# A decoder block in one kernel: residual rows tied to the block sums, two operand sums split by VectorE, split left operands of two more FFN2 products, another token order in the last product

## The chip, the cores and the metric

One core of one Trainium2 chip. The metric is device time of one launch in microseconds (us); the kernel was run three times before the change. Names: TensorE (PE) multiplies, VectorE (DVE), ScalarE (ACT) and GpSimd (POOL) do elementwise work, SyncE (SP) issues nearly all DMAs. PSUM is the memory that TensorE writes its products to.

## The reference, cut to what matters

```python
x = layer_norm(ALPHA * x + gate1 * mixer(...), ln1_g, ln1_b)      # x: 1024 tokens x 1024, float32
...
h = x * (1 + scale2) + shift2                                     # 1024 x 1024
u = h @ ffn_w_up                                                  # 1024 x (2 * 2816): gate and value halves
u = causal_dwconv(u, ffn_conv) + ffn_conv_b                       # 3 taps per channel
a = silu(u[:, :2816]) * u[:, 2816:]
y = a @ ffn_w_down                                                # 1024 x 1024
out = layer_norm(ALPHA * x + gate2 * y, ln2_g, ln2_b)
```

The mixer (gated DeltaNet and GLA heads, two thirds of the program before the FFN) is not touched by the change.

## The kernel before, in words

**Arithmetic.** Each float32 matmul is made of three matmuls on parts: an operand is split into a rounded high part `hi` (a cast by ScalarE) and a low part `lo` = value − hi (a subtraction by DVE or GpSimd). `hi*lo`, `lo*hi` and `hi*hi` are summed in PSUM. Both FFN multiplications are block products of Winograd's kind: seven products with the numbers 1 to 7 take the place of eight, and operands and results are sums and differences of blocks.

**FFN1** (`w_up`). Channels come in 22 blocks `f` of 128; each block has the seven products, each 12 matmuls of 128x512. The activations' sums S1 to S4 (for products 5, 6, 7, 3) are made once and split once, into `s1h/s1l`, `s2h/s2l`, `s3h/s3l`, `s4h/s4l` (`s_rows`, `split_s`): S1 and S2 by ScalarE and DVE, S3 and S4 by ScalarE and GpSimd. The weights' sums are made and split per block by the generator `weights(f)`: tiles `vq` (value part), `wst` (gate part), split into `vh/vl` by `split_q`; product 4's weight sum `wq[f]` is a cell of `acc`, for f = 0 the tile `B22` of product 3, so that its sum comes after product 3's split. `carry(f, i)` takes what a product leaves in PSUM to the next: copies by ScalarE (`p1_`, `p4_`, `p5_`, `u2_`), sums by DVE (`add_p1` at L1456, L1477, L1479, L1481), the convolution `conv` (ScalarE L1400, two DVE instructions L1403), SiLU (L1460) and the product with the gate (L1461).

**Between the two.** After every second block the generator `sums(j)` makes the left operands of FFN2 from a pair of blocks and stores them to DRAM: products 1, 5 and 3 whole (`dS`), products 6, 7, 2 and 4 in two parts by `put_split` (`dSp`, L1410 ScalarE, L1411 DVE or GpSimd). `residual_rows(n)` scales 16 half tiles (128 tokens x 512) of the first LayerNorm's output for the last residual: load (L1447), two DVE instructions (L1449, L1450), store (L1451). Two cells of `acc` take turns.

**FFN2** (`w_down`). Products in the order 1, 5, 6, 3, 7, 2, 4; each has 11 entries (`entry`) of a left and a right operand, in a ring of eight slots of `aH/aL`, and for every entry four token tiles of three matmuls. The right operand is loaded (`R0`, `R1`, `bt`), cast by ScalarE (L1614) and split by DVE (L1615). A left operand that was stored in two parts is loaded right into its slot; one that was stored whole is loaded to `st`, cast by ScalarE (L1617) and split by GpSimd (L1618). `collect` and `done` (L1666 to L1670) take the results out of PSUM, `ln2` normalises them. In the last product, token tiles are gone through one after the other; tiles 0 and 1 lie in one PSUM tile, 2 and 3 in another, the last in two halves of 256 columns.

**What sets the order.** TensorE's order is the program's (`manual_schedule`). The order on DVE, ScalarE, GpSimd and SP is set by a scheduler that places each instruction where it expects its inputs, so code that is written late in the loop may stand early in a queue: the 16 pairs of residual instructions, written one per block from f = 4 on, all ran between 739.9 and 840.6 us. Each engine works through its queue in order.

## Time and profile before

| | |
|---|---|
| three runs | 1469.51, 1470.5, 1473.1 us; median 1470.5 |
| profiled execution | 1465.25 us, its span 1463.5 us |
| busy | PE 1333.3 us (91%), DVE 1013.6 (69%), ACT 591.9 (40%), POOL 577.1 (39%) |
| mean granted clock of TensorE | 0.949 of full |

The span is the time from the first to the last instruction of the profiled execution; FFN1 proper begins at some 740 us and FFN2 at 1210 us of it. A timeline row has start and duration in us, engine, line and operation, tiles (out<-in) and, in brackets, how long the engine had been idle and what ended that. Lines are those of the kernel before; in the change they lie 2 to 11 lines further down (L1352 becomes L1363, L1449 L1451, L1456 L1458, L1614 L1616).

### The profile page before, as it was taken

How to read it: one execution, taken by the hardware profiler on the slowest of the kernel's cores; microseconds unless marked ns; L12 is line 12 of the kernel's file. 1: busy time of each engine (PE TensorE's matmuls, PEld its weight loads, DVE VectorE, ACT ScalarE, POOL GpSimd, SP SyncE). 2: the span in 40 equal slices, each digit the busy share in tenths (PEclk: the TensorE clock that was granted, in tenths of full speed). 3: DMA queues.
4: the chain of work that ended last, by engine and by line, in shares of the span. 5: the costliest groups of instructions: out<-in, count | busy, mean ns of one | idle time of the engine just before them, and what ended most of it. 6: DMA issues, size and time to landing. Idle time of an engine off the chain costs nothing.

```text
span 1463.5 us, 19001 instructions
## 1 busy us (share of the span) xinstructions
PE 1333.3 (91%) x6662; PEld 1059.5 (72%) x6662; DVE 1013.6 (69%) x1756; ACT 591.9 (40%) x957; POOL 577.1 (39%) x383
## 2 busy tenths in 40 slices
PE   6796999999998999999957799999999997799995
PEld 4564777777787777777846587777888775688875
DVE  7885954587458334874587888878788878832777
ACT  4356222233234432532653354544445445333221
POOL 2674211121116865442352544444544435612006
PEclk9888999999999998999988999999999998899998
DMA  9546212131204554252324643334444329775773
GB/s 317 150 150 203 71 25 57 32 72 55 67 9 122 167 186 137 93 187 89 114 87 150 202 129 99 115 118 137 137 137 137 113 81 351 233 241 165 263 242 116
DMA packets 192406, 203.39 MB, mean 139 GB/s; under 512 B 29748, under 2 KB 124848, under 8 KB 192310
## 3 DMA queue, kind: packets, MB, share of 16 engines
q1 hardware_dynamic: 192021, 201.12, 43.2%
q8 instruction: 53, 0.87, 0.2%
q10 hardware_dynamic: 288, 1.05, 0.2%
q14 instruction: 44, 0.35, 0.1%
HBM read 147.04 MB, written 55.09 MB: 138 GB/s over the span
## 4 chain that ended last, share of the span: by engine, by line
PE 53%; DVE 19%; issue 9%; DMA 8%; POOL 6%; ACT 4%; SPq 0%; POOLq 0%; DVEq 0%; ACTq 0%
PE up L1281 13%; PE pp L622 6%; PE pp L623 5%; PE pp L624 5%; PE up L1633 4%; PE up L1634 4%; PE up L1632 4%; DMA vq<-in_ffn_w_up 3%; DVE ob L1403 2%; DMA K<-in_w_ada 1%; PE dn L864 1%; DVE mac L236 1%; DVE vl L1306 1%; POOL vl L1306 1%; POOL wlo L158 1%
## 5 line engine op out<-in xcount | busy, mean ns | idle before, releaser
L622 PE MATMUL pp<-aH,wlo 128*128 128x512 f32 x432 | 191.1, 442 | 8.7 <-DVE ob L651 6.9
L158 POOL TENSOR_TENSOR wlo<-wst,whi 128x1024 fp32r<-128x1024 f32 x50 | 125.5, 2510 | 153.9 <-ACT whi L157 152.5
L623 PE MATMUL pp<-aL,whi 128*128 128x512 f32 x432 | 176.5, 409 | 0.0
L624 PE MATMUL pp<-aH,whi 128*128 128x512 f32 x432 | 176.4, 408 | 0.0
L1306 POOL TENSOR_TENSOR vl<-vq,vh 128x512 fp32r<-128x512 f32 x44 | 73.3, 1666 | 175.0 <-ACT vh L1305 164.5
L1632 PE MATMUL up<-aL,aH 128*128 128x512 f32 (+1 forms) x304 | 119.5, 393 | 19.2 <-ACT aH L1617 11.4
L1633 PE MATMUL up<-aH,aL 128*128 128x512 f32 (+1 forms) x304 | 119.3, 392 | 8.5 <-POOL aL L1618 8.5
L1403 DVE SCALAR_TENSOR_TENSOR ob<-up,colC,ob 128x1023 f32<-128x1023 f32 (+1 forms) x88 | 112.2, 1276 | 20.8 <-ACT ob L1400 20.2
L1634 PE MATMUL up<-aH 128*128 128x512 f32 (+1 forms) x304 | 118.7, 391 | 0.0
L622 PEld LDWEIGHTS pp<-aH,wlo 128*128 128x128 f32 x432 | 84.9, 196 | 30.8 <-DVE ob L651 5.8
L624 PEld LDWEIGHTS pp<-aH,whi 128*128 128x128 f32 x432 | 84.7, 196 | 20.6
L623 PEld LDWEIGHTS pp<-aL,whi 128*128 128x128 f32 x432 | 85.7, 198 | 14.5 <-issue 0.5
L157 ACT CAST whi<-wst 128x1024 fp32r<-128x1024 f32 x50 | 52.3, 1047 | 83.4 <-PE pp L624 28.1
L1618 POOL TENSOR_TENSOR aL<-st,aH 128x512 fp32r<-128x512 f32 x33 | 55.5, 1698 | 76.4 <-ACT aH L1617 76.4
L1400 ACT ACTIVATE ob<-up,colC 128x1024 f32<-128x1024 f32 x44 | 53.0, 1207 | 80.6 <-DVE up L1479 47.7
L1615 DVE TENSOR_TENSOR aL<-R,aH 128x512 fp32r<-128x512 f32 x63 | 47.2, 757 | 54.5 <-ACT aH L1614 54.3
L1632 PEld LDWEIGHTS up<-aL,aH 128*128 128x128 f32 x304 | 58.9, 194 | 32.6 <-ACT aH L1617 12.3
L1281 PE MATMUL up<-aH,vl 128*128 128x512 f32 x176 | 70.9, 403 | 11.7 <-DVE vl L1306 11.0
L1614 ACT CAST aH<-R 128x512 fp32r<-128x512 f32 x63 | 39.0, 621 | 102.2 <-PE up L1634 88.4
L1633 PEld LDWEIGHTS up<-aH,aL 128*128 128x128 f32 x304 | 58.8, 194 | 20.8 <-POOL aL L1618 9.3
L1281 PE MATMUL up<-aH,wlo 128*128 128x512 f32 x176 | 70.7, 401 | 1.9 <-ACT ob L1469 1.0
L1281 PE MATMUL up<-aL,vh 128*128 128x512 f32 x176 | 70.4, 400 | 0.0
(519 smaller groups left out, 3476.4 us busy)
## 6 DMA issues: line engine op xcount, KB each, us to landing
wst<-in_w_in SPq DMA_DIRECT2D x28, 512.0 KB
K<-in_w_ada SPq DMA_DIRECT2D x48, 256.0 KB, 2.9
wst<-in_ffn_w_up SPq DMA_DIRECT2D x22, 512.0 KB, 4.4
vq<-in_ffn_w_up SPq DMA_DIRECT2D x44, 256.0 KB, 4.0
dS<-ob SPq DMA_DIRECT2D x33, 256.0 KB, 2.1
R<-in_ffn_w_down SPq DMA_DIRECT2D x33, 256.0 KB, 5.5
st<-dS SPq DMA_DIRECT2D x33, 256.0 KB, 4.7
wada<-in_w_ada SPq DMA_DIRECT2D x8, 1024.0 KB, 8.7
```

The costliest lines, as they stand in the source:

```text
L158: eng.tensor_tensor(lo, st, hi.bitcast(F32), op=ALU.subtract)
L622: PE.matmul(pp, lo[:, k, :], aH[:, k, sl], start=(k == 0), stop=False)
L623: PE.matmul(pp, hi[:, k, :], aL[:, k, sl], start=False, stop=False)
L624: PE.matmul(pp, hi[:, k, :], aH[:, k, sl], start=False, stop=(k == NK - 1))
L1281: PE.matmul(o, w[:, k, :], a, start=flags[0], stop=flags[1], skip_group_check=not first_)
L1306: eng.tensor_tensor(lo, q, hi.bitcast(F32), op=ALU.subtract)
L1400: S.activation(t, cb, AF.Identity, bias=w(3), scale=w(2))
L1403: V.scalar_tensor_tensor(t[:, sh:], cb[:, :T - sh], w(j), t[:, sh:], op0=ALU.mult, op1=ALU.add)
L1618: G.tensor_tensor(lo[:, HS[0]], s, hi[:, HS[0]].bitcast(F32), op=ALU.subtract)
L1632: PE.matmul(pb, l_hi, r_lo, start=new, stop=False, skip_group_check=i not in (1, 5, 2))
L1633: PE.matmul(pb, l_lo, r_hi, start=False, stop=False, skip_group_check=i not in (1, 5, 2))
L1634: PE.matmul(pb, l_hi, r_hi, start=False, stop=(j == NJ - 1), skip_group_check=i not in (1, 5, 2))
```

## The change

Six edits. (1) In `weights(0)` the weight sum of product 4 gets a `vq` tile of its own and is made and split ahead of product 3's split; the call of `weights(0)` is moved ahead of `h2_of(NT - 2)`. (2) S3 and S4 are split by DVE, and their casts and splits are issued after the last cast and split of S1 and S2. (3) The two residual instructions of a half tile are issued after the sum of product 3 (`anchor`) of the latest block. (4) Products 1 and 5 are stored in two parts, product 6 whole; the order in `sums` follows from that. (5) The rows of gamma and beta of the last LayerNorm are loaded in product 3's place of the loop, not ahead of FFN2. (6) The last product takes the token tiles in the order 0, 2, 1, 3.

```diff
         split_q(f, 6, B12, V)
         yield
+        wq[f] = t4_ if f else ft([P, 4, P], "vq", 3)
+        if f == 0:
+            V.tensor_tensor(wq[f], st[:, KH[1], :], B12, op=ALU.subtract)
+            split_q(f, 4, wq[f], V)
         split_q(f, 3, B22)
         yield
-        wq[f] = t4_ if f else B22
-        V.tensor_tensor(wq[f], st[:, KH[1], :], B12, op=ALU.subtract)
+        if f:
+            V.tensor_tensor(wq[f], st[:, KH[1], :], B12, op=ALU.subtract)
         V.tensor_tensor(B12, B12, st[:, KH[0], :], op=ALU.subtract)
         split_q(f, 7, B12)
...
     with tc.manual_schedule(engines={PE.engine}):
         load_w(0)
-        h2_of(NT - 2)
-        product(1, 1)
         ahead = weights(0)
         next(ahead)
         next(ahead)
+        h2_of(NT - 2)
+        product(1, 1)
         next(ahead)
-        next(ahead, None)
-        split_q(0, 4, wq[0], V)
...
         for i in (5, 6):
-            s_rows(i, 0, 2, V)
-            s_rows(i, 2, 3, V)
-            s_rows(i, 3, 4, V)
-        s_rows(3, 0, 4, G)
-        for r0, r1 in ((0, 3), (3, 4)):
-            s_rows(7, r0, r1, G)
+            for r0, r1 in ((0, 2), (2, 3), (3, 4)):
+                split_last = s_rows(i, r0, r1)
+        next(ahead, None)
+        for i, rows in ((3, ((0, 4),)), (7, ((0, 3), (3, 4)))):
+            for r0, r1 in rows:
+                with tc.issue_after(split_last[0].ins), tc.issue_after(split_last[1].ins):
+                    s_rows(i, r0, r1)
...
-    dS = {i: dram.tile([NJ, P, 512], F32, name=f"dS{i}") for i in (1, 5, 3)}
-    dSp = {i: [dram.tile([NJ, P, 512], F32, name=f"dS{i}{s}") for s in "hl"] for i in (6, 7, 2, 4)}
+    dS = {i: dram.tile([NJ, P, 512], F32, name=f"dS{i}") for i in (6, 3)}
+    dSp = {i: [dram.tile([NJ, P, 512], F32, name=f"dS{i}{s}") for s in "hl"] for i in (1, 5, 7, 2, 4)}
...
-        nc.sync.dma_start(dS[1][j], a11)
         put_split(4, j, a22, V)
         yield
-        put_split(2, j, a12, G)
+        put_split(1, j, a11, V)
         V.tensor_tensor(a22, a21, a22, op=ALU.add)
-        nc.sync.dma_start(dS[5][j], a22)
         V.tensor_tensor(a21, a11, a21, op=ALU.subtract)
         yield
+        put_split(5, j, a22, G)
         V.tensor_tensor(a11, a22, a11, op=ALU.subtract)
-        put_split(6, j, a11, G)
+        nc.sync.dma_start(dS[6][j], a11)
         yield
         put_split(7, j, a21, G)
+        yield
+        put_split(2, j, a12, G)
...
-        V.tensor_tensor(r, r, g1h[0], op=ALU.mult)
-        V.tensor_tensor(r, r, b1h[0], op=ALU.add)
+        with tc.issue_after(anchor[0].ins):
+            V.tensor_tensor(r, r, g1h[0], op=ALU.mult)
+            V.tensor_tensor(r, r, b1h[0], op=ALU.add)
...
-            V.tensor_tensor(v[:, 0, :], v[:, 0, :], u2_, op=ALU.add)
+            anchor[0] = V.tensor_tensor(v[:, 0, :], v[:, 0, :], u2_, op=ALU.add)
...
-    g2r, b2r = rows_of(2, ln2_g[0], ln2_b[0])
+    ln2_rows = []
...
+                if i == 3 and j == 0:
+                    ln2_rows.extend(rows_of(2, ln2_g[0], ln2_b[0]))
...
-        for t in range(4):
+        for t in (0, 2, 1, 3):
```

The order on the engines moves with it, at three places.

DVE at the start of FFN1, before; `vl_6338` is the low half for product 4's weights, `s1l` and `s2l` those of S1 and S2, L1449 and L1450 residual rows:

```order
L1343 TENSOR_TENSOR vq_6275<-vq_6275,wst_6230 128x512
L1352 TENSOR_TENSOR s1l_6341<-ob,aH 128x512
L1243 TENSOR_TENSOR gate<-ob,gate 128x512
L1352 TENSOR_TENSOR s1l_6341<-gate,aH 128x512
L1244 TENSOR_TENSOR ob<-ob 128x512
L1449 TENSOR_TENSOR ob<-ob,g1h_7006 128x512
L1244 TENSOR_TENSOR ob<-gate,ob 128x512
L1306 TENSOR_TENSOR vl_6338<-vq_6276,vh_6337 128x512
L1245 TENSOR_TENSOR ob<-ob 128x512
L1450 TENSOR_TENSOR ob<-ob,b1h_7009 128x512
L1352 TENSOR_TENSOR s2l_6343<-ob,s2h_6342 128x512
```

The same place in the change; `vl_6330` is now the low half for product 4, `wst_6529` the gate weights of f = 2:

```order
L1347 TENSOR_TENSOR vq_6275<-vq_6275,wst_6230 128x512
L1243 TENSOR_TENSOR ob<-ob 128x512
L1363 TENSOR_TENSOR s1l_6337<-ob,aH 128x512
L1242 TENSOR_TENSOR gate<-gate 128x512
L1458 TENSOR_TENSOR up_6314<-up_6314,ob 128x512
L1333 TENSOR_TENSOR vq_6440<-vq_6440,wst_6236 128x512
L1244 TENSOR_TENSOR ob<-ob 128x512
L1243 TENSOR_TENSOR gate<-ob,gate 128x512
L1363 TENSOR_TENSOR s1l_6337<-gate,aH 128x512
L1245 TENSOR_TENSOR ob<-ob 128x512
L1333 TENSOR_TENSOR vq_6525<-vq_6525,wst_6529 128x512
L1244 TENSOR_TENSOR ob<-gate,ob 128x512
```

The split of product 4 stands in the row ahead of these; the residual rows are gone; the weight sums L1333 of f = 1 and f = 2 have come in ahead of the S2 splits; then S3 and S4 follow on DVE:

```order
L1363 TENSOR_TENSOR s2l_6339<-ob,s2h_6338 128x512
L1336 TENSOR_TENSOR vq_6440<-vq_6441,vq_6440 128x512
L1363 TENSOR_TENSOR s3l_6342<-ob,aL 128x1536
L1363 TENSOR_TENSOR s3l_6342<-gate,aL 128x512
L1346 TENSOR_TENSOR ob<-wst_6236,vq_6440 128x512
L1363 TENSOR_TENSOR s4l_6341<-ob,s4h_6340 128x2048
L1306 TENSOR_TENSOR vl_6477<-vq_6440,vh_6476 128x512
```

They stood in GpSimd's queue before.

DVE at the end of a block in the middle of FFN1, before; L1333 is the next weights' sum, L1456 `add_p1`, whose result TensorE waits for:

```order
L1403 SCALAR_TENSOR_TENSOR ob<-up_7384,colC,ob 128x1023
L1403 SCALAR_TENSOR_TENSOR ob<-up_7384,colC,ob 128x1022
L1333 TENSOR_TENSOR vq_7697<-vq_7697,wst_7701 128x512
L1456 TENSOR_TENSOR up_7508<-up_7508,ob 128x512
L1403 SCALAR_TENSOR_TENSOR ob<-up_7368,colC,ob 128x1023
```

In the change, with the residual rows L1451 and L1452 of that block:

```order
L1458 TENSOR_TENSOR up_7677<-up_7677,ob 128x512
L1333 TENSOR_TENSOR vq_7849<-vq_7849,wst_7853 128x512
L1403 SCALAR_TENSOR_TENSOR ob<-up_7519,colC,ob 128x1023
L1306 TENSOR_TENSOR vl_7757<-vq_7711,vh_7756 128x512
L1403 SCALAR_TENSOR_TENSOR ob<-up_7519,colC,ob 128x1022
L1433 TENSOR_TENSOR ob<-ob 128x512
L1336 TENSOR_TENSOR vq_7711<-vq_7712,vq_7711 128x512
L1479 TENSOR_TENSOR up_7695<-up_7695,ob 128x512
L1451 TENSOR_TENSOR ob<-ob,g1h_7009 128x512
L1463 TENSOR_TENSOR ob<-ob 128x1024
L1346 TENSOR_TENSOR ob<-wst_7715,vq_7711 128x512
L1452 TENSOR_TENSOR ob<-ob,b1h_7012 128x512
```

The sum stands ahead of L1333 in all blocks but f = 2, 3, 4 and 21 (before, it did in about every second one), and the residual rows behind the sum of product 3.

ScalarE at the start of FFN2, before; L1400 is the convolution of the last block, L1614 the right operands' cast, L1617 the left ones':

```order
L1460 ACTIVATE ob<-ob 128x1024
L1400 ACTIVATE ob<-up_9479,colC 128x1024
L1614 CAST aH<-R_9623 128x512 x3
L1400 ACTIVATE ob<-up_9463,colC 128x1024
L1614 CAST aH<-R_9623 128x512 x3
L1460 ACTIVATE ob<-ob 128x1024
L1617 CAST aH<-st_9626 128x512
L1617 CAST aH<-st_9633 128x512
```

In the change:

```order
L1400 ACTIVATE ob<-up_9509,colC 128x1024
L1400 ACTIVATE ob<-up_9491,colC 128x1024
L1616 CAST aH<-R_9654 128x512 x6
L1462 ACTIVATE ob<-ob 128x1024
L1616 CAST aH<-R_9654 128x512 x2
```

The left operands' casts are gone from here, and both activations stand ahead of the first right operand.

## Rows read from the trace of the kernel before

**Rows 1.** Waits of TensorE, 640 to 1464 us: line, what it waited for, total, times, longest.

```profile
PE up L1281 <- DVE up L1456: 15.3, 5, 7.4
PE up L1632 <- ACT aH L1617: 11.4, 2, 10.1
PE up L1281 <- DVE vl L1306: 11.0, 1, 11.0
PE up L1633 <- POOL aL L1618: 8.5, 2, 7.9
PE up L1632 <- DVE ob L1666: 7.8, 3, 5.7
PE up L1281 <- ACT ob L1471: 6.5, 1, 6.5
PE up L1281 <- POOL s4l L1352: 3.9, 1, 3.9
```

**Rows 2.** Windows: length; busy PE, PEld, DVE, ACT, POOL; granted clock, DMA share, GB/s.

```profile
752.70:758.30 5.60, 5.49 (x12) 3.81 (x12) 3.01 (x6) 3.28 (x3) 5.60 (x1) 0.50 0.17 48
919.00:998.00 79.00, 78.28 (x337) 62.76 (x336) 63.41 (x67) 39.62 (x56) 37.78 (x23) 1.00 0.39 127
1220.00:1252.00 32.00, 30.18 (x121) 24.03 (x121) 29.61 (x30) 14.87 (x27) 20.50 (x13) 0.90 1.02 371
```

**Rows 3.** Timeline of TensorE at the start of FFN1.

```profile
752.76 0.80 PE L1281 MATMUL up<-aH,vl 128*128 128x512 f32 x1 [10.98 <-DVE vl L1306]
...
768.89 0.79 PE L1281 MATMUL up<-s4l,vh 128*128 128x512 f32 x1 [3.86 <-POOL s4l L1352]
...
773.83 0.49 PE L1281 MATMUL up<-aL,vl 128*128 128x512 f32 x1 [0.65 <-ACT ob L1473]
...
788.94 0.77 PE L1281 MATMUL up<-s4h,vl 128*128 128x512 f32 x1 [6.54 <-ACT ob L1471]
```

**Rows 4.** Timeline of DVE at the start of FFN1.

```profile
744.20 0.68 DVE L1306 TENSOR_TENSOR vl<-vq,vh 128x512 fp32r<-128x512 f32 x1
...
755.03 0.68 DVE L1352 TENSOR_TENSOR s2l<-ob,s2h 128x512 fp32r<-128x512 f32 x1
...
764.50 4.88 DVE L1450 TENSOR_TENSOR ob<-ob,b1h 128x512 f32<-128x512 f32 x1
...
782.48 0.69 DVE L1449 TENSOR_TENSOR ob<-ob,g1h 128x512 f32<-128x512 f32 x1 [2.63 <-DMA ob<-ax]
```

**Rows 5.** Timelines of GpSimd and ScalarE at the start of FFN1.

```profile
749.47 9.58 POOL L1352 TENSOR_TENSOR s3l<-ob,aL 128x1536 fp32r<-128x1536 f32 x1 [6.35 <-ACT aL L1351]
...
763.88 4.95 POOL L1352 TENSOR_TENSOR s4l<-ob,s4h 128x2048 fp32r<-128x2048 f32 x1
...
752.52 1.05 ACT L157 CAST whi<-wst 128x1024 fp32r<-128x1024 f32 x1 [0.97 <-DMA wst<-in_ffn_w_up]
```

**Rows 6.** Timeline of DVE at the end of a block.

```profile
896.45 2.20 DVE L1333 TENSOR_TENSOR vq<-vq,wst 128x512 f32<-128x512 f32 x1 [3.56 <-DMA vq<-in_ffn_w_up]
```

**Rows 7.** Groups of DVE: the two residual instructions; count, busy, mean ns, idle before.

```profile
L1450 DVE TENSOR_TENSOR ob<-ob,b1h 128x512 f32<-128x512 f32 x16 | 18.1, 1130 | 0.1
...
L1449 DVE TENSOR_TENSOR ob<-ob,g1h 128x512 f32<-128x512 f32 x16 | 14.2, 887 | 15.6 <-DMA ob<-ax 15.6
```

**Rows 8.** Timelines of ScalarE and DVE at the start of FFN2.

```profile
1209.67 0.62 ACT L1614 CAST aH<-R 128x512 fp32r<-128x512 f32 x1 [4.67 <-DMA R<-in_ffn_w_down]
...
1212.53 1.20 ACT L1400 ACTIVATE ob<-up,colC 128x1024 f32<-128x1024 f32 x1
...
1219.13 2.63 ACT L1617 CAST aH<-st 128x512 fp32r<-128x512 f32 x4 [0.55 <-DMA st<-dS]
...
1213.76 1.28 DVE L1403 SCALAR_TENSOR_TENSOR ob<-up,colC,ob 128x1023 f32<-128x1023 f32 x1 [0.41 <-ACT ob L1400]
```

**Rows 9.** Timeline of DVE at the end of the program.

```profile
1450.26 0.42 DVE L1666 TENSOR_TENSOR ob<-up,gate 128x256 f32<-128x256 f32 x1 [0.75 <-PE up L1634]
...
1454.98 0.42 DVE L1666 TENSOR_TENSOR ob<-up,gate 128x256 f32<-128x256 f32 x1 [3.19 <-PE up L1634]
```

More of the change, by code (lines that the diff above doesn't have):

```diff
@@ L1347, in build, with s_rows @@
     parts_s = {}
-    def split_s(i, src, rows, eng):
-        hi, lo = parts_s[i]
-        S.copy(hi[:, rows, :], src)
-        eng.tensor_tensor(lo[:, rows, :], src, hi[:, rows, :].bitcast(F32), op=ALU.subtract)
-    def s_rows(i, r0, r1, eng):
+    def s_rows(i, r0, r1):
         rows = slice(r0, r1)
@@ L1361, in s_rows @@
             src = acc[:, 4 + r0:4 + r1, HS[i == 5]]
-        split_s(i, src, rows, eng)
+        hi, lo = parts_s[i]
+        return (S.copy(hi[:, rows, :], src),
+                V.tensor_tensor(lo[:, rows, :], src, hi[:, rows, :].bitcast(F32), op=ALU.subtract))
     with tc.manual_schedule(engines={PE.engine}):
         load_w(0)
-        h2_of(NT - 2)
-        product(1, 1)
         ahead = weights(0)
@@ L1448, in residual_rows @@
         yield
-        V.tensor_tensor(r, r, g1h[0], op=ALU.mult)
-        V.tensor_tensor(r, r, b1h[0], op=ALU.add)
+        with tc.issue_after(anchor[0].ins):
+            V.tensor_tensor(r, r, g1h[0], op=ALU.mult)
+            V.tensor_tensor(r, r, b1h[0], op=ALU.add)
         nc.sync.dma_start(d, r)
-    pending = []
+    pending, anchor = [], [None]
     def add_p1(f):
@@ L1646, in ln2 @@
         o = acc[:, t, :]
+        g2r, b2r = ln2_rows
         mv = sm([P, 2], "bmv")
```

## The prediction, made before the changed kernel was run

> **What bounds the kernel now.** I read the waits of TensorE in the last 820 us first. There the reader sees seven named waits that make 64.4 us in sum [rows 1]; outside them TensorE hardly stops. The windows come next: in the steady part of the first FFN product, four blocks of f take 79 us and TensorE is busy for 78.3 of them, so one of their 28 products lasts 2.82 us and only the matmuls themselves bound that stretch [rows 2]. So the time to win lies in the stalls, at four places: the start of FFN1, the sums at the end of some f, the start of FFN2 and of its product 5, and the last product. A stall costs more than its idle time: after the 10.98 us stall the next twelve matmuls ran at a granted clock of 0.50 and took 5.5 us, 2.7 more than a product at full clock [rows 2, 3].
>
> **The sum** is made against the profiled execution (1465.25 us, a span of 1463.5 and 1.75 around it). It is 5.25 us below the median, 1470.5; the forecast is the median less the gain.
>
> **Part 1, start of FFN1.** TensorE waits for the low half of the weights of product 4 until 752.76, for s4l of product 3 until 768.89 and for an evacuation by ScalarE until 788.94 [rows 3]. The low halves of S3 and S4 were made by GpSimd, one of them in a 9.58 us record that starts at 749.47, the other only at 763.88 [rows 5]; and residual instructions of DVE stand ahead of the last S2 split, which starts at 755.03; another waits for its DMA until 782.48, ahead of the sums that release the last stall [rows 4]. After the change the weight split of product 4 stands where a split of DVE started at 744.20 [rows 4], some 8 us earlier. That is not all gained, because product 5 is then held by p4's copy, which ScalarE's order has behind a weight cast; that cast waits for a load until 752.52 [rows 5]. The load was issued behind a residual store and load which are gone, so I estimate the cast at 750 to 752 and product 5 at 752 to 754. Next come two splits of S2, which now stand behind a sum that needs the same load: 753 to 755. Then S3 and S4 on DVE: 4096 columns at 0.60 to 0.68 per 512 [rows 4] are 4.9 to 5.4 us, with a split, a subtraction and a sum of 0.68 each between them. S4 is ready at about 761 to 763, against 768.8. From s4l to the start of product 7 the trace has 4.94 us, part of it at low clock, and from there three products, 8.5 us, to the stall at 788.94 [rows 2, 3]: 761.5 + 4.9 + 8.5 = 775. The last stall was made by the residual load, which is gone; the two 1024-wide activations ahead of the copy stay. Gain 788.9 − 775 = 14, and 1 us of low clock after that stall: **15** (bounds 8 to 20: with the load as late as before, or with no wait left but s4l).
>
> **Part 2, the sums of a block.** Five stalls end with the sum at L1456, 15.3 us, one of them 7.4, so the other four are 1.97 each [rows 1]. In one of these, DVE waited 3.56 us for a weight load, then took 2.20 us for L1333, and only then came L1456 [rows 6]. The change's order puts L1456's successor ahead of L1333 in every block but f = 2, 3, 4 and 21, and the residual rows behind the sum of product 3. I leave two stalls of 1.97, 0.8 for f = 21 and 1 for DVE's higher load; with 1.5 us of low clock behind the long one, half of the 2.7 above, that gives 15.3 + 1.5 − 3.9 − 0.8 − 1 = **11** (bounds 4 to 16). The load on DVE: 16 pairs of residual instructions, 0.89 + 1.13 us [rows 7], are no longer bunched but come one pair per block, and each pair of blocks has one more split by DVE (0.68 to 1.3) and one more cast of ScalarE. DVE was busy 63.4 of 79 us [rows 2], so it has 3.9 us free per block and gets 2.0 + 0.3 to 0.7. That fits, with 1.2 to 1.6 left. Twelve writes of 256 KB per pair instead of eleven are hidden: the DMA engines were 0.39 busy [rows 2].
>
> A rule speaks against this. First the row: L1450, a residual addition of 0.68 us alone, took 4.88 us at 764.50, while GpSimd ran s4l from 763.88 to 768.83; it ended 0.55 us after it [rows 4, 5]. The Trainium skill, "SBUF — State Buffer", section "SBUF: two separate sides", says that a VectorE instruction with two SBUF inputs and a GpSimd instruction that reads SBUF take a shared port pair as an exclusive lock, so that the later one waits for the whole of the other. The row agrees. By that rule the added pair, both with two SBUF inputs, can each stand behind one whole GpSimd instruction instead of the mean that I used, and a block could overrun; that is the first rival, below. In the sum I keep the two means, since they were taken beside GpSimd work too. The same two rows are why moving S3 and S4 off GpSimd frees DVE as well.
>
> **Part 3, start of FFN2.** The 10.1 us [rows 1] run from the last product of FFN1 to 1219.8. The right operand's cast had come at 1209.67; the cast of the left one came at 1219.13, waiting for its load [rows 8]. Now the left operands of product 1 lie in DRAM in two parts and the first four entries are loaded ahead. What stays: the ScalarE activations of the last block (1.20 each) and a DVE one (1.28) ahead of the first cast and split (0.62, 0.68) [rows 8], behind the last product's sum: two activations, cast, DVE step, split = 2.4 + 0.6 + 1.3 + 0.7 = 5. Gain 5, and about 1 for a shorter run at low clock: **6** (bounds 4 to 9). The gamma and beta rows, which SP's order now has in product 5, cost nothing; the 31 us of product 5 (11 x 2.82) hide them.
>
> **Part 4, product 5.** GpSimd made the low halves of its left operands; that wait is 8.5 us, 7.9 of it at once [rows 1]. They are read ready-made now. What may stay is the right operand's cast, 1.3 us of the L1617 group. With 1 us of low clock I take **9** (bounds 7 to 11). Reads grow by 11 x 256 KB, 0.71 us each at the 371 GB/s of the stretch [rows 2], 7.8 us of transfers beside 62 us of two products. A product-1 or product-5 entry needs 768 KB, 2.1 us, and four tokens of matmuls take 2.8, so they stay hidden; the second rival is that they don't. Product 6 gets the casts and GpSimd splits that product 5 loses, but eight entries ahead.
>
> **Part 5, last product.** Tokens 0, 2, 1, 3 put a whole group (2.8 us a product x 11 / 4 = 7.8) between two uses of a PSUM tile, so the waits for L1666, 7.8 us [rows 1], go from TensorE. But DVE's normalisations are not fewer, and from 1421 to the last matmul DVE was idle only 0.75 + 3.19 us [rows 9]. So DVE decides the end and gives **4** (bounds 2 to 8, the upper if its order also meets GpSimd less).
>
> **Sum:** 15 + 11 + 6 + 9 + 4 = 45; 1470.5 − 45 = **1425.5**.
>
> **Rivals.** (a) *DVE becomes the bound in the blocks.* For: the lock row, 0.80 of the time busy already. Against: 3.9 us free per block. Priced at 1.97 per block, by the four stalls where one instruction too many stood ahead of the sum: in 8 of the 16 residual blocks 16 us more, 1441; in all of them 32, 1457. Chance 0.15, most of it the first. (b) *DMA at the start of FFN2.* For: share 1.02 in 1220 to 1252, the engines were full [rows 2]. Against: much of that was prefetch that nobody waited for. The 7.8 us of added transfers then fall into products 1 and 5: 1433. Chance 0.1. (c) *The start is not shortened as ordered*: S3 and S4 are on DVE but behind the sum that waits for the load; if that load still lands at 752.5 and the casts follow in ScalarE's queue, part 1 gives its lower end 8: 1432.5. Chance 0.1. (d) *Slower:* the residual store waits on SP's queue for DVE, and the next blocks' weight loads stand behind it; each block's L1333 waits 3.56 us for such a load already [rows 6]. If a late pair delays the loads by its own wait and DVE's sum then comes after it, every block pays. The other parts give 34, and part 2 starts from 16.8 already in the time, so the kernel is slower from (34 + 16.8) / 16 = 3.2 us per block; at 3.56 + 0.6 it is 1470.5 − 50.8 + 66.6 = 1486. Against: the loads are issued a block ahead. Chance 0.05. The forecast has 0.6.
>
> **How the numbers follow.** The parts' lower bounds together give 25, 1445.5, the upper ones 64, 1406.5; not all are hit at once. Rivals (b), (c) and most of (a) lie inside 1408 to 1446; left out are the worse half of (a), (d) and the far ends. A measurement can tell some 0.3%, 4.4 us, from no change. Faster 0.93, within 0.3% 0.02, slower 0.05, which is (d).
>
> **What would show it.** Right: no wait over 4 us between FFN1's start and its end; the s4l wait on DVE, not GpSimd; L1458 without DMA waits ahead of it in the blocks; DVE near 0.9 busy in a four-block window with TensorE still at 78 of 79; a first FFN2 stall of 4 to 6; no GpSimd wait in product 5; TensorE's last matmul some 13 us before the end of the span, not 8.5 as now [rows 9]. Wrong: a wait of 1 to 4 us in each block, a product-1 or 5 entry waiting for DMA, or a new wait of product 5 of FFN1 beyond 756.

## The result, and the profile after

The changed kernel takes **1446.36 us** (median of four runs, 1443.91 to 1447.75) against 1471.8 for the kernel before on the same chip (1469.51 to 1473.68): a ratio of 0.983, interval 0.980 to 0.985. It is 25 us faster; the prediction was 45, and its range ended just below the result. The profiled executions are 1447.39 us (span 1445.7) and 1465.25 (span 1463.5), 17.8 us apart in span: that of before lies 6.5 us under its median, that of after 1 us above. The account by parts below is of the spans, so some 7.5 us of the difference between the medians have no place in it.

TensorE's waits, with the columns of [rows 1]:

```profile
PE up L1281 <- ACT ob L1471: 14.1, 8, 2.5
PE up L1634 <- DVE ob L1669: 7.1, 1, 7.1
PE up L1281 <- DVE up L1458: 6.5, 3, 3.2
PE up L1281 <- DVE vl L1306: 4.2, 1, 4.2
PE up L1634 <- issue: 4.1, 1, 4.1
PE up L1281 <- DVE up L1481: 2.3, 1, 2.3
...
PE up L1281 <- DVE s4l L1363: 1.3, 1, 1.3
```

The waits at the start of FFN1, 11.0 and 6.5 us, at the start of FFN2, 10.1, and near the end of its product 1, 7.9, have shrunk as meant [rows 1]. A new one leads the list: eight times in the blocks TensorE waits for a copy of ScalarE, L1471. The windows of the steady part, columns of [rows 2], show that it costs more than its 14.1 us:

```profile
840.00:919.00 79.00, 74.58 (x309) 60.13 (x310) 66.16 (x71) 36.15 (x53) 33.32 (x20) 0.96 0.40 134
919.00:998.00 79.00, 75.17 (x324) 60.43 (x323) 66.55 (x74) 39.18 (x56) 34.85 (x22) 1.00 0.48 159
```

TensorE was busy for 78.28 of the second window before [rows 2], now for 75.17. A block should take seven products of some 2.8 us [rows 2]. From one start of product 3 to the next TensorE's timeline gives 19.4 to 20.2 before for all but three of the steady blocks (21.7); after the change nearly every second one takes 21.4 to 25.6. FFN1 from its second product 3 to its end takes 434.3 us instead of 420.7 (its last matmul ends at 1210.83; before, at 1209.68). So the 12.4 us won at its start (the second product 3 begins at 776.55 instead of 788.94) are lost again by its end, and the whole gain in span, 17.8, stems from FFN2.

Here is one such block. DVE's timeline (start, duration; in brackets idle time and what ended it), from the sum `add_p1` (L1458) on:

```profile
881.52 0.70 DVE L1458 TENSOR_TENSOR up<-up,ob 128x512 f32<-128x512 f32 x1
886.18 2.58 DVE L1333 TENSOR_TENSOR vq<-vq,wst 128x512 f32<-128x512 f32 x1 [3.96 <-DMA vq<-in_ffn_w_up]
888.68 1.27 DVE L1403 SCALAR_TENSOR_TENSOR ob<-up,colC,ob 128x1023 f32<-128x1023 f32 x1
...
893.06 0.69 DVE L1479 TENSOR_TENSOR up<-up,ob 128x512 f32<-128x512 f32 x1
893.66 0.68 DVE L1451 TENSOR_TENSOR ob<-ob,g1h 128x512 f32<-128x512 f32 x1
894.26 2.31 DVE L1463 TENSOR_TENSOR ob<-ob 128x1024 f32<-128x1024 f32 x1
...
897.70 0.68 DVE L1481 TENSOR_TENSOR up<-up,ob 128x512 f32<-128x512 f32 x1
```

and ScalarE's and TensorE's timelines there:

```profile
898.42 1.20 ACT L1400 ACTIVATE ob<-up,colC 128x1024 f32<-128x1024 f32 x1 [1.20 <-DVE up L1481]
899.52 0.57 ACT L1471 COPY ob<-up 128x512 f32<-128x512 f32 x1
...
900.15 0.50 PE L1281 MATMUL up<-aH,wlo 128*128 128x512 f32 x1 [2.05 <-ACT ob L1471]
```

L1333 makes a weights' sum ahead of time: TensorE's next product 5 (from 895.17 on) still uses the sum that the L1333 of the block before made, and this one is needed only by the product 5 after it. It stands behind `add_p1`, as the prediction had it, but one row ahead of the convolution, and waits 3.96 us for a load. From 882.2 to 897.7 DVE pauses only there, and then works through its backlog: convolution (L1403), L1479, a residual row, the gate product, L1481. L1481 is late, so ScalarE's L1400 and L1471 are, and TensorE stands. The wait that TensorE shows names none of the instructions that began it. Of DVE's own waits from 840 to 1180 us, those of L1333 (total, times, longest) were these before:

```profile
DVE vq L1333 <- DMA vq<-in_ffn_w_up: 25.1, 10, 3.6
DVE vq L1333 <- POOL ob L1411: 13.4, 7, 2.7
```

and these after:

```profile
DVE vq L1333 <- DMA vq<-in_ffn_w_up: 36.0, 14, 5.5
DVE vq L1333 <- POOL vl L1306: 2.3, 1, 2.3
DVE vq L1333 <- POOL gate L1411: 1.2, 1, 1.2
```

In the seven waits that name GpSimd before, a load for the same instruction landed within 0.1 us of the end of GpSimd's, so the profile cannot tell the two apart. Taken together L1333 waits 38.5 us in 17 times before and 39.5 in 16 after: the wait did not grow, it moved in front of other instructions.

### The profile page after: what moved, and what is told of

It reads as the page before. It is cut to its first block, busy times and chain, and to the rows that moved or that the text cites. A ratio compares the mean times of both kernels' runs of the same rounds, so it can differ in the third digit from the quotient of the medians.

```text
span 1445.7 us, 19012 instructions
## 1 busy us (share of the span) xinstructions
PE 1337.2 (92%) x6662; PEld 1061.9 (73%) x6662; DVE 1005.0 (70%) x1770; ACT 590.1 (41%) x957; POOL 532.9 (37%) x369
## 3 DMA queue, kind: packets, MB, share of 16 engines
q10 hardware_dynamic: 288, 1.05, 0.2%
## 4 chain that ended last, share of the span: by engine, by line
PE 50%; DVE 23%; DMA 10%; issue 9%; POOL 4%; ACT 3%; SPq 1%; POOLq 0%; DVEq 0%; ACTq 0%
PE up L1281 9%; PE pp L622 6%; PE pp L623 5%; PE pp L624 5%; PE up L1634 4%; PE up L1636 4%; PE up L1635 4%; DMA vq<-in_ffn_w_up 3%; DVE ob L1403 2%; DVE vq L1333 1%; POOL vl L1306 1%; PE dn L864 1%; DVE mac L236 1%; DMA K<-in_w_ada 1%; DVE vl L1306 1%
## 5 line engine op out<-in xcount | busy, mean ns | idle before, releaser
L158 POOL TENSOR_TENSOR wlo<-wst,whi 128x1024 fp32r<-128x1024 f32 x50 | 122.6, 2452 | 160.0 <-ACT whi L157 159.5
L1306 POOL TENSOR_TENSOR vl<-vq,vh 128x512 fp32r<-128x512 f32 x44 | 70.2, 1595 | 213.3 <-ACT vh L1305 209.0
L1634 PE MATMUL up<-aL,aH 128*128 128x512 f32 (+1 forms) x304 | 118.7, 391 | 11.8 <-DVE ob L1669 7.1
L1403 DVE SCALAR_TENSOR_TENSOR ob<-up,colC,ob 128x1023 f32<-128x1023 f32 (+1 forms) x88 | 112.2, 1276 | 20.8 <-ACT ob L1400 19.5
L624 PEld LDWEIGHTS pp<-aH,whi 128*128 128x128 f32 x432 | 84.9, 196 | 20.6
L623 PEld LDWEIGHTS pp<-aL,whi 128*128 128x128 f32 x432 | 85.5, 198 | 14.5 <-issue 0.5
L1281 PE MATMUL up<-aH,wlo 128*128 128x512 f32 x176 | 74.0, 420 | 17.4 <-ACT ob L1471 14.1
L1617 DVE TENSOR_TENSOR aL<-R,aH 128x512 fp32r<-128x512 f32 x63 | 44.1, 705 | 51.9 <-ACT aH L1616 51.8
L1281 PE MATMUL up<-aH,whi 128*128 128x512 f32 x176 | 71.9, 409 | 0.0
L1281 PE MATMUL up<-aL,whi 128*128 128x512 f32 x176 | 71.7, 407 | 0.0
L1281 PE MATMUL up<-aH,vh 128*128 128x512 f32 x176 | 70.1, 398 | 0.0
```

The source lines that it names most:

```text
L158: eng.tensor_tensor(lo, st, hi.bitcast(F32), op=ALU.subtract)
L623: PE.matmul(pp, hi[:, k, :], aL[:, k, sl], start=False, stop=False)
L624: PE.matmul(pp, hi[:, k, :], aH[:, k, sl], start=False, stop=(k == NK - 1))
L1281: PE.matmul(o, w[:, k, :], a, start=flags[0], stop=flags[1], skip_group_check=not first_)
L1306: eng.tensor_tensor(lo, q, hi.bitcast(F32), op=ALU.subtract)
L1403: V.scalar_tensor_tensor(t[:, sh:], cb[:, :T - sh], w(j), t[:, sh:], op0=ALU.mult, op1=ALU.add)
```

## The experiments

Two theories. **A:** the pair of residual rows, now between L1479 and L1481 in each block, lengthens the chain to L1471 (from the sum of product 3, now L1479, to that of product 7, now L1481, it was 3.44 us before; after, 4.64 in the block above). **D:** L1333's wait in DVE's queue is the cost, the pair only adds to it. Edits are to the changed kernel, unless said otherwise; every ratio is to the kernel before, run beside it. The medians of the kernel before in these groups of runs lie between 1466.4 and 1473.5 us, so a difference in us between runs of two groups is uncertain by some us.

**Pair and L1333 behind `add_p1`** (e1). The pair is tied to `add_p1`, and L1333 is kept behind an `add_p1`.

```diff
+    anchor, sums_done = [None], []
...
-        V.tensor_tensor(B12, B12, st[:, KH[0], :], op=ALU.subtract)
+        with ExitStack() as late:
+            if len(sums_done) > 1:
+                late.enter_context(tc.issue_after(sums_done[-2].ins))
+            V.tensor_tensor(B12, B12, st[:, KH[0], :], op=ALU.subtract)
...
-    pending, anchor = [], [None]
+    pending = []
...
-        V.tensor_tensor(gp[f][:, 0, :], gp[f][:, 0, :], p1_, op=ALU.add)
+        anchor[0] = V.tensor_tensor(gp[f][:, 0, :], gp[f][:, 0, :], p1_, op=ALU.add)
+        sums_done.append(anchor[0])
...
-            anchor[0] = V.tensor_tensor(v[:, 0, :], v[:, 0, :], u2_, op=ALU.add)
+            V.tensor_tensor(v[:, 0, :], v[:, 0, :], u2_, op=ALU.add)
```

> Edit to the changed kernel: the residual pair is tied to the sum after product 2 (add_p1), where VectorE waits for the next weights' load, no longer to the sum of product 3; the next weights' sum (L1333) stays behind add_p1, as in the changed kernel. Theory A (the pair, 1.3 us, stands on the chain L1479, L1481, ScalarE's L1400, copy L1471 that TensorE waits for): the L1471 waits of TensorE, 14.1 us in 8 stalls, fall to 5 us or less, the interval from the one sum to the other falls from 4.6 or 5.2 us to 3.4 as it was before the change, and the time falls by 8 to 14 us, to 1432 to 1438. Theory B (the loads for L1333 come late, whatever stands in the chain): L1333 waits 3 to 5 us as now, the L1471 stalls stay at 10 us or more, time within 4 us of 1446.

1463.59 us, ratio 0.994 (0.991 to 0.996): 17 slower than the change, which neither theory had forecast. With the pair off the chain, L1479 to L1481 takes 3.44 us again and TensorE's waits for ScalarE's copy fall to 7.5 us, but the blocks got worse: every second one now takes 23.5 to 25.4 us, and TensorE waits for the convolution itself (21.6 us). L1333, the pair and the last FFN2 subtraction now all stand ahead of it, and L1333 still waits, 27.2 us in 16 times. So the shorter chain alone is no gain; but since the pair only took another early place in the same queue, this run does not tell A from D.

**Pair behind product 7's sum** (e2).

```diff
+        yield
...
-            anchor[0] = V.tensor_tensor(v[:, 0, :], v[:, 0, :], u2_, op=ALU.add)
+            V.tensor_tensor(v[:, 0, :], v[:, 0, :], u2_, op=ALU.add)
...
-            V.tensor_tensor(v[:, 1, :], g[:, 1, :], p5_, op=ALU.add)
+            anchor[0] = V.tensor_tensor(v[:, 1, :], g[:, 1, :], p5_, op=ALU.add)
```

> Edit: the pair is tied to the sum of product 7 (L1481 of the changed kernel), so it stands behind the chain; but the scheduler then puts the next weights' sum (L1333) ahead of add_p1 again in most blocks. Theory A: no L1471 stall over 1 us; in its place waits for add_p1 of about 2 us in the blocks where L1333's load is late, so 1436 to 1444. Theory B: the stalls only change their name: the sum over both names stays at 15 to 22 us and the time within 4 us of 1446.

1485.0 us, ratio 1.008 (1.006 to 1.010), 39 slower than the change and far from both forecasts. The scheduler, given another tie, put L1333 ahead of `add_p1` in most blocks, and TensorE waited 40.8 us, 16 times, for that sum.

**No residual rows** (e3). This kernel leaves out the scaling of the residual rows altogether.

```diff
-                        pending.append(residual_rows(f - 4))
+                        pass
```

> The 16 residual half tiles are left out (not loaded, scaled or stored, so the last residual adds the unscaled rows): what they cost at all in FFN1, on VectorE and on the DMA queue. Theory A: the L1471 stalls are under 4 us in sum and the time is 1428 to 1438; L1333 still waits 2 to 4 us for its load. Theory B, in the form that the pair's 8 MB of loads and stores delay the weights: L1333's waits fall under 1.5 us and the time is 1428 to 1436 too, with no wait for add_p1 left.

1483.84 us, ratio 1.008 (1.005 to 1.011). With 32 DVE instructions, their loads and stores gone the kernel is 37 us *slower*, where both theories had it faster: L1333 again stands mostly ahead of `add_p1` (37.9 us in 18 waits for it). What A called the cost is gone here, and nothing is won; the place of L1333 outweighs it.

**Stores as before** (e4): edit 4 undone, edit 5 kept.

```diff
-    dS = {i: dram.tile([NJ, P, 512], F32, name=f"dS{i}") for i in (6, 3)}
-    dSp = {i: [dram.tile([NJ, P, 512], F32, name=f"dS{i}{s}") for s in "hl"] for i in (1, 5, 7, 2, 4)}
+    dS = {i: dram.tile([NJ, P, 512], F32, name=f"dS{i}") for i in (1, 5, 3)}
+    dSp = {i: [dram.tile([NJ, P, 512], F32, name=f"dS{i}{s}") for s in "hl"] for i in (6, 7, 2, 4)}
...
+        nc.sync.dma_start(dS[1][j], a11)
...
-        put_split(1, j, a11, V)
+        put_split(2, j, a12, G)
...
```

> Edit to the changed kernel: products 1 and 5 stored whole and 6 in two parts, in the old order of the sums generator; the residual pair stays on the sum of product 3. Theory A: the stalls on L1471 stay at 8 us or more, and FFN2 loses what it gained (a stall of 6 to 10 us at its start and one of 6 to 9 at product 5): 1455 to 1465. Theory C (the twelfth store and the extra split, not the pair, overfill the blocks): L1471 stalls under 4 us and FFN1's end 8 to 12 us earlier, so that the time is within 5 us of 1446 in spite of FFN2's stalls.

1460.97 us, ratio 0.9945 (0.991 to 0.998): 14.6 slower than the change, nearly the 15 that parts 3 and 4 were priced at. The waits of FFN2 return (GpSimd's `aL` 9.2 us, ScalarE's `aH` 6.4), and the blocks are no better (438.0 us from the second product 3 to the end, 434.3 with the change). Taking the added stores away does not shorten the blocks. What they cost by themselves this run cannot say, since L1333 moved too: it stands ahead of `add_p1` in every second block, as in the kernel before, and TensorE waits 11.6 us for that sum beside 11.8 for ScalarE's copy.

**L1333 a block later in DVE's queue** (e5): the edit that tells D.

```diff
-    wq, loaded = {}, {}
+    wq, loaded, sums_done = {}, {}, []
...
-        V.tensor_tensor(B12, B12, st[:, KH[0], :], op=ALU.subtract)
+        with ExitStack() as late:
+            if sums_done:
+                late.enter_context(tc.issue_after(sums_done[-1].ins))
+            V.tensor_tensor(B12, B12, st[:, KH[0], :], op=ALU.subtract)
...
-        V.tensor_tensor(gp[f][:, 0, :], gp[f][:, 0, :], p1_, op=ALU.add)
+        sums_done.append(V.tensor_tensor(gp[f][:, 0, :], gp[f][:, 0, :], p1_, op=ALU.add))
```

> Edit to the changed kernel: the weights' first sum (L1333) of a block is tied to add_p1 of the block before it, which puts it one block later in VectorE's queue, behind the arrival of its loads; nothing else is moved. In the changed kernel it stands a block ahead of its first use, waits 1 to 5.5 us for its load and holds the rest of VectorE's queue. Theory D (that in-order wait is what TensorE pays for in the blocks, under the names L1471, L1458 or L1403): L1333 waits less than 1 us, the three names together fall from 22 us to under 5, time 1418 to 1430. Rival E (the ring of three weight tiles bounds the blocks: load, sum, splits, next load): the wait moves to TensorE waiting for the split of product 5 (vl, L1306), 10 us or more in sum, time 1440 to 1452.

**1424.84 us**, ratio 0.968 (0.965 to 0.971), 21.5 faster than the change. Its windows:

```profile
840.00:919.00 79.00, 78.50 (x340) 63.42 (x339) 66.70 (x76) 40.55 (x58) 36.76 (x22) 1.00 0.48 160
919.00:998.00 79.00, 78.02 (x337) 62.72 (x336) 64.48 (x75) 40.20 (x58) 35.34 (x22) 1.00 0.50 167
```

DVE has as much to do as in the change (66.70 against 66.16, 64.48 against 66.55), the pair is where it was, DMA moves more, and TensorE is busy 3 to 4 us more of each 79. DVE's timeline at the end of a block (L1461 is `add_p1`, L1336 the late sum, L1406 the convolution):

```profile
893.75 0.69 DVE L1461 TENSOR_TENSOR up<-up,ob 128x512 f32<-128x512 f32 x1
894.35 1.17 DVE L1336 TENSOR_TENSOR vq<-vq,wst 128x512 f32<-128x512 f32 x1
897.72 1.28 DVE L1406 SCALAR_TENSOR_TENSOR ob<-up,colC,ob 128x1023 f32<-128x1023 f32 x1 [2.20 <-ACT ob L1403]
```

L1336 stands at the same place, but is now the sum whose load has had a block more time, and does not wait at all. TensorE's waits for the copy, for `add_p1` and for the convolution are 6.6 us together (forecast: under 5). FFN1 from the second product 3 to its end is 411.7 us. D holds. A by itself is refuted: the pair sits between L1482 and L1484 here as well, and they lie 4.64 or 5.25 us apart in the steady blocks, as in the change. Two things left with the early place: the waits, and time of the instruction itself, whose 22 executions take 35.9 us in the change and 22.0 here. How the gain divides between these two was not measured.

**That edit on the kernel before** (e7). The same diff in the kernel before.

> The same edit as e5 alone, on the kernel before. Theory D: the four 1.95 us waits for L1456 go (6 to 8 us), the 7.45 us one, made by a residual load, stays or shrinks: 1460 to 1465. Rival E: within 3 us of the kernel before.

1455.89 us, ratio 0.989 (0.986 to 0.992): 14.5 faster by this alone, more than forecast. From the fourth on, the blocks take 19.4 to 20.2 us, and the waits for `add_p1` [rows 1] fall to 5.3 in two. TensorE waits 17.0 us instead of 11.0 for product 4's weights at the start of FFN1, but from FFN1's first matmul to the second product 3 it takes 60.3 us against 60.9 before, so nothing is lost there.

The sixteen blocks from the fifth start of product 3 to the twenty-first put the cases side by side: 313.3 us with neither pair nor wait (e7), 316.9 with the pair and the added stores (e5), 319.7 with L1333's wait alone (the kernel before, whose last pair ended at 844.8), 331.3 with pair, stores and wait (the change), and 346.1 with pair and wait, without the stores and with L1333 in the order of before (e4). So the pair is not free: beside the wait it goes with 11.6 us or more, without it with 3.6 at most. The change put the two together.

**No tie** (e8) and **no tie, with the late L1333** (e11): edit 3 undone, in the change and in e5.

```diff
-        with tc.issue_after(anchor[0].ins):
-            V.tensor_tensor(r, r, g1h[0], op=ALU.mult)
-            V.tensor_tensor(r, r, b1h[0], op=ALU.add)
+        V.tensor_tensor(r, r, g1h[0], op=ALU.mult)
+        V.tensor_tensor(r, r, b1h[0], op=ALU.add)
```

> The changed kernel without the tie of the residual pairs (edit 3 undone): the scheduler hoists the pairs to the start of FFN1 again. Theory D: the tie itself did not help the blocks; L1333 stands where its load is late in either order, so the blocks lose 10 to 30 us as in the other variants, 1445 to 1475, and the start of FFN1 loses some of its gain. My prediction's part 2: without the tie the blocks are as in the kernel before, with 15 us of waits, and the start loses 5 or more: 1450 to 1460.

> e5 without the tie of the residual pairs: the pairs are hoisted to the start of FFN1. If the tie matters by itself: FFN1's first blocks lose 8 us or more to the pairs and their loads (waits for add_p1, as the 7.45 us one before the change), 1433 to 1445. If only the place of the weights' sum mattered, within 3 us of e5's 1424.8.

1487.3 us (1.011, 1.009 to 1.014) and 1453.36 us (0.988, 0.984 to 0.992). Without its tie the change is 41 us slower, with 39.5 us of waits for `add_p1`, behind L1333. Both results lie outside all forecasts. So edit 3 is worth more than edits 4 and 6, the others that were undone by themselves, and much of that through the place of L1333 that comes with it. That this is not all shows in e11: L1333 does not wait there, and the kernel is still 28.5 us behind e5.

**Token order as before** (e10).

```diff
-        for t in (0, 2, 1, 3):
+        for t in range(4):
```

> The changed kernel with the last product in the old token order 0, 1, 2, 3. My prediction's part 5: 4 us slower, 1448 to 1452, with waits for L1669 of 1.5 and 5.7 us. Rival: the order 0, 2, 1, 3 only moved the wait to between the halves of the last tile (7.1 us) and the time is within 2 us of 1446.4.

1446.82 us (0.983, 0.979 to 0.987), 0.5 from the change: edit 6 is worth nothing that these runs can tell. With the old order TensorE waits 7.8 us for L1669 in three waits, as before [rows 1], with the new one 7.1 in one.

**Another order for the last product** (e6, on e5): tiles 2, 0, the first half of 3, 1, the second half of 3.

```diff
-        for t in (0, 2, 1, 3):
-            for sl in (HS[0],) if t < 3 else (slice(0, 256), slice(256, 512)):
-                for j in range(NJ):
-                    matmuls(on1[t][:, sl], 4, j, t, sl)
...
+        for t, sl in ((2, HS[0]), (0, HS[0]), (3, slice(0, 256)), (1, HS[0]), (3, slice(256, 512))):
+            for j in range(NJ):
+                matmuls(on1[t][:, sl], 4, j, t, sl)
...
```

> e5 and another order of the last product: token tiles 2, 0, first half of 3, 1, second half of 3, so that no PSUM tile is written again right after it was read. If the 7.1 us wait for L1669 between the halves of tile 3 costs time at the end: the wait falls under 1 us and the time is 2 to 4 us under e5, since VectorE was idle for only 3.6 us there. If VectorE's normalisations alone set the end: within 1.5 us of e5.

**1416.8 us** (1416.3 to 1417.64), ratio 0.963 (0.961 to 0.965), the best of all and faster than both kernels. The 7.1 us wait is gone; FFN2 takes 226.7 us from its first matmul to the end of the span, against 230.6 in e5 and 230.4 to 232.7 in the other runs with FFN2 as in the change, so 3.9 of the 8 us between the two come from this edit. The other 4 lie in FFN1, which the edit does not touch (407.5 against 411.7 us); e5's runs alone are 4.6 us apart.

**Pair behind product 7's sum, on e6** (e9, the diffs of e2 and e6), and then **the last FFN2 subtraction on GpSimd** (e12):

```diff
-        V.tensor_tensor(a12, a12, a11, op=ALU.subtract)
+        G.tensor_tensor(a12, a12, a11, op=ALU.subtract)
```

> e6 with the residual pair tied to the sum of product 7 instead of product 3, so that its 1.3 us stand behind the chain L1479, L1481, L1400, L1471, with the weights' sum kept late. Theory A, now as a remainder (the pair on that chain is what is left of the waits for the copy L1471, 4.4 us in 5 stalls in e6): they fall under 1 us, time 2 to 6 us under e6, 1411 to 1415. If the pair costs nothing there: within 2 us of e6's 1416.8.

> The version with the late weight sum, the other token order and the residual pair tied to product 7's sum (1448.7 us) with one more edit: the last subtraction of `sums` (a12 - a11, product 3 of FFN2), one 0.7 us instruction per pair of blocks, is done by GpSimd in place of DVE. In that version this subtraction stands on DVE ahead of the two convolution instructions L1406 and waits there for GpSimd's split of the same rows, 33.6 us in eight waits; in the version at 1416.8 us it stands behind them and hardly waits. Theory F (the 32 us between the two are this one instruction's place in DVE's in-order queue): without it the convolution starts when ScalarE's L1403 ends, 1.1 to 3 us earlier in each second block, TensorE's waits for DVE ob L1406 and ACT ob L1475 (10.5 and 14.9 us) fall below 6 together, and the time is 1416 to 1426. Theory G (the pair behind product 7's sum is itself what delays the block, or ScalarE's wait for a store in front of L1403 does): these waits stay and the time is 1440 to 1452.

e9 takes 1448.68 us (0.984, 0.979 to 0.989), 32 slower than e6 (29 when each is held against the kernel before beside it), and its expectation is missed. Its DVE shows the pattern of the change with another instruction (L1436 is that subtraction; L1483 stands for L1479):

```profile
937.82 1.61 DVE L1336 TENSOR_TENSOR vq<-vq,wst 128x512 f32<-128x512 f32 x1
944.73 2.88 DVE L1436 TENSOR_TENSOR ob<-ob 128x512 f32<-128x512 f32 x1 [5.29 <-POOL ob L1414]
947.53 1.27 DVE L1406 SCALAR_TENSOR_TENSOR ob<-up,colC,ob 128x1023 f32<-128x1023 f32 x1
...
951.83 0.69 DVE L1483 TENSOR_TENSOR up<-up,ob 128x512 f32<-128x512 f32 x1
```

L1436 may overwrite its rows only once GpSimd has split them, and GpSimd waits for stores of the two cells that take turns (3.74 us from 933.85 on, 1.56 from 941.84). In e6 it stands behind both L1406 and hardly waits; here it stands ahead of them, 33.6 us of waits in eight. e12, which gives this one instruction to GpSimd, takes **1423.37 us** (0.971, 0.967 to 0.975): 25 us back, as its Theory F said, or 18 when each is held against the kernel before beside it, which was 7 us faster in this group. TensorE's waits for L1406 are gone from its list, those for ScalarE's copy are 9.6 us where up to 6 were expected for both. The pair is off the chain here (L1483 to L1485 takes 3.44 us), and these waits are still not below the 4.4 us of e6, where it is on it. In e11 L1436 waits 27.2 us at the same place; that this is e11's loss was not tried apart.

## Why the prediction was wrong

The sign was right, the size was not: 45 was forecast, the medians give 25. By steps, from the spans:

- **Part 1, start of FFN1: 15 forecast, 12.4 measured.** Of this, FFN1's first matmul already starts 1.6 us later (729.60, before 728.02), behind a part that the change does not touch; counted from there the gain is 14.0 (12.4 in the profile of e10, which has the same start). The order of events was as described. S4's low half was ready when TensorE used it at 765.58, forecast 761 to 763, because the second S2 split came at 759.17, 4 us later than forecast (1.6 of them the later start). Moving S3 and S4 to DVE held its price: 4.71 us in three instructions against 4.9 to 5.4 (eight times 0.60 is 4.8, a slip).

```profile
760.38 1.75 DVE L1363 TENSOR_TENSOR s3l<-ob,aL 128x1536 fp32r<-128x1536 f32 x1
762.05 0.68 DVE L1363 TENSOR_TENSOR s3l<-gate,aL 128x512 fp32r<-128x512 f32 x1
...
763.25 2.28 DVE L1363 TENSOR_TENSOR s4l<-ob,s4h 128x2048 fp32r<-128x2048 f32 x1
```

- **Part 2, the sums of a block: +11 forecast, −13.6 measured. This step failed**, by 24.6 of the 27.2 us that the spans miss. It read [rows 6] as "L1333 stands one place too early" and took the wait away once `add_p1` was ahead; for what stands behind L1333 it has no term. But DVE works through its queue in order: moved behind `add_p1`, L1333 still waited for its load (39.5 us, 38.5 before), and the wait passed to what came next, the convolution and through it L1479, L1481 and ScalarE's L1471, a chain that the pair had made longer. The Trainium skill, "PSUM — Partial Sum Buffer", section "Engine vs sequencer instructions", says that VectorE's queue is strictly first in, first out; the row at 886.18 agrees, with a backlog that follows its wait without a gap. With the sum made a block later (e5) part 2 measures 420.7 − 411.7 = +9.0, and the whole gain is 45.5 against the kernel before beside it, 39.6 in the spans: the sum of 45 was near that of a kernel in which L1333 never waits in the blocks.
- **Part 3, start of FFN2: 6 forecast, 7.0 measured** (from the end of FFN1 to product 1's tenth entry). The stall fell from 10.13 to 4.05 us, and the first entry behind it takes 5.26 us instead of 6.21. What ends the 4.05 us the profile does not name.

```profile
1214.88 0.77 PE L1634 MATMUL up<-aL,aH 128*128 128x512 f32 x1 [4.05 <-issue]
```

- **Part 4, product 5: 9 forecast, 10.1 measured, at another place.** The prediction read the waits of 7.9 and 1.3 us as product 5's, and the 1.3 as one for a right operand. They stood one after the other at the last of the eleven entries of product 1, which begins at 1219.81, and L1617 casts left operands. TensorE's and GpSimd's timelines of the kernel before:

```profile
1252.00 0.50 PE L1632 MATMUL up<-aL,aH 128*128 128x512 f32 x1 [1.27 <-ACT aH L1617]
1260.40 0.79 PE L1633 MATMUL up<-aH,aL 128*128 128x512 f32 x1 [7.90 <-POOL aL L1618]
1252.02 8.33 POOL L1618 TENSOR_TENSOR aL<-st,aH 128x512 fp32r<-128x512 f32 x1 [7.80 <-ACT aH L1617]
```

  That edit 4 also covers product 1's entries is why the gain came all the same; that the size fits is luck. The split that TensorE waited for has a record of 8.33 us, against 1.27 at the shortest, and DVE was busy for 8.37 of the 8.40 us from 1252.0 to 1260.4, with 13 subtractions in a row. In e4 two such splits take 11.36 us from 1253.13 on, beside a DVE busy for 8.77 of the 8.80 us from 1254.0 to 1262.8. So the size of that wait seems to lie in what DVE did beside GpSimd, a term that the prediction does not have; no run tests it by itself. With the operands stored in two parts no wait above 0.4 us is left there, and of the reads that were added TensorE sees waits under 1 us in all.

- **Part 5, the last product: 4 forecast, 1.9 measured from product 6 on, and 0.5 when undone by itself (e10).** Neither is more than the spread of 2.3 us between the runs with this FFN2. "DVE decides the end" was right, but the wait was counted as gone from TensorE, when it only moved: the two halves of tile 3 follow each other in one PSUM tile, and DVE, with hardly a gap from 1414.72 to 1434, reaches the first half's sum only at 1431.57.

```profile
1432.05 0.58 PE L1634 MATMUL up<-aL,aH 128*128 128x256 f32 x1 [7.08 <-DVE ob L1669]
```

The parts give 12.4 − 13.6 + 7.0 + 10.1 + 1.9 = 17.8, the difference of the spans.

Of the rivals, (a) gave 1441 to 1457, and the result lies there, but not by its mechanism: DVE's load did not decide, since e5 carries it at 78 of 79 us. (b) and (c) did not come about. (d) named L1333's wait, but let `add_p1` come after it; with that order the change would indeed have been slower than before, as e2, e3 and e8 are (1484 to 1487, forecast 1486). That the number fits is luck: (d) blamed the residual store for the late load, and e3 has no residual store.

The rule of the Trainium skill that the prediction weighed ("SBUF — State Buffer", section "SBUF: two separate sides") shows again: L1333 above took 2.58 us, and 0.68 at its shortest; GpSimd's instruction there was

```profile
885.80 2.41 POOL L158 TENSOR_TENSOR wlo<-wst,whi 128x1024 fp32r<-128x1024 f32 x1 [3.69 <-ACT whi L157]
```

and L1333 ended 0.55 us after it (888.76 against 888.21), the same 0.55 as in [rows 4, 5]. The overrun of a block that the rule could have meant for the added pair did not come, and the mean of 0.89 and 1.13 us was too high: each of the 32 instructions of the pairs takes 0.68 in the change. In e5, with a pair in each of sixteen blocks, the blocks after the start take 19.4 to 20.6 us, but for two of 21.4 and 22.6.

Of the prediction's signs of being wrong one came, "a wait of 1 to 4 us in each block", in about every second block. Of its signs of being right, TensorE's last matmul was to end some 13 us before the span does; it ends 8.0 before it, and 13.1 in e6, where the wait between the halves is gone.

## What to carry to other kernels

In an in-order queue, ask of every instruction that waits for a DMA not only who needs it, but who stands behind it: an early place is free only if its operand has landed. A forecast that moves such an instruction must move its wait along, to the next in the queue. And where a scheduler sets the order, an edit's worth may lie in what else it shifts, so compare the whole queue around each moved row, and tie the waiting instruction itself. A change that adds work behind such an instruction pays for both: here the pair and the wait cost far more together than the pair without the wait.

## What was not expected of the hardware

Nothing new about the chip was needed to explain the result. What surprised is how far order alone goes: kernels with nearly the same instructions lie between 1416.8 and 1487.3 us, and one with 32 DVE instructions fewer is 37 us slower (e3). In the start of FFN2 the DMA engines moved 392 GB/s, against 371 in [rows 2], at a share that the profile gives as 1.05:

```profile
1215.00:1247.00 32.00, 32.00 (x131) 26.23 (x132) 26.88 (x42) 12.59 (x21) 9.34 (x2) 0.92 1.05 392
```

TensorE was busy throughout those 32 us, so a full DMA stretch delayed nothing there, which is what spoke against rival (b).

One row of the kernel before stands out: GpSimd's split of 8.33 us beside a DVE without a pause (part 4). The 9.58 us record of S3 in [rows 5] has the same company: DVE worked without a gap until 755.71, and the record ends 3.3 us later.
